# Query, key and value products of two chunks at a time, with seven block products in place of eight

## The chip, the core and the metric

The kernel runs on one core of a Trainium2 chip. The metric is the device time of one execution in microseconds (us), from the first to the last instruction on the core. TensorE is called PE here, VectorE DVE, ScalarE ACT, GpSimd POOL; SP is the engine whose queue issues nearly all transfers.

## What is computed

A two-layer encoder over 2048 frames of 1024 features, in float32. Cut to what matters:

```python
# layer A: pooling mixer, output projection, gated embedding
x = x + pool_mixer(rms_norm(x, a_norm), a_w_in, a_w_group, a_scale, a_w_out)
x = x + (p[0] @ ple_w[0]) * sigmoid(x @ ple_gate_w[0])
# layer B: one key/value projection, queries, stick-breaking attention
k, v = split(rms_norm(x, kv_norm) @ w_kv)          # 1024 -> 1024 each
q, z = split(rms_norm(x, b_norm) @ b_w_in)         # 1024 -> 1024 each
k, q = rms_norm(heads(k), k_norm), rms_norm(heads(q), b_q_norm)   # 16 heads of 64
beta = sigmoid(q @ k.T / 8)                        # strictly causal
A[t, s] = beta[t, s] * prod(1 - beta[t, j] for s < j < t)
x = x + ((A @ v) * silu(z)) @ b_w_out
x = x + (p[1] @ ple_w[1]) * sigmoid(x @ ple_gate_w[1])
```

## The kernel before, in words

The 2048 frames are four chunks of 512 (`NSUB`, `W5`). Every dense product is done in three matmuls: the activations and the weights are each split into a rounded high part and the rest (`split`, `put_split`: ACT casts the high part, DVE or POOL subtracts it), and high·high, low·high and high·low are summed in PSUM.

**Weights** come in units of 256 columns by two row blocks, or 512 columns by one, in a fixed order (`plan`). `pump` loads the next unit as soon as one of nine buffers (`UNITS`, line 29) is given back, so loads run up to nine units ahead of PE. A unit is 12 matmuls of work. The first time a unit is used its raw form (256 KB) is loaded and split on the chip; where it will be used again its split form (512 KB) is stored (`once`, `keep=True`) and loaded from there later.

**One chunk's front half**: `mixer` (mixer products; in chunk 0 also `fold`, which multiplies weights together), `out_steps` (output projection), `gate_steps` (gate and embedding), `gate_z` and `kvq`. `kvq` (line 690) makes q, k or v of one half of the columns: activations stand still as 128 x 128 blocks and 512 weight columns stream, 8 row blocks x 4 token blocks x 3 matmuls. Per chunk that is 3 kinds x 2 halves x 96 = 576 matmuls. `keyed` (line 757) then scales a token block of k or q by its norm, sums squares per head, takes the power -1/2 on POOL (`rsqrt_mean`, line 162; 8 heads, so 8 columns at a time) and multiplies; after the fourth token block four jobs `finish(m)` are put in `lag`, the first due 34 PE steps later, in which PE transposes the rows and the result is split and stored. `valued` and `differences` store v and make differences of neighbouring rows.

**Attention** goes by slots (chunk, head, key chunk), two half-steps each. In a half-step PE does `gather` (matmuls of weights `at` with `vv` into `pso`), `turn` (8 transposes of an older half-step's `pp` into `psa`), `front` (4 matmuls into `psl`); ACT makes the sigmoid `pp` and the high part of `at`; DVE subtracts for the low part of `at` (line 984) and runs the product scan over `pp` (line 964), two of each per half-step. `turn` lags `front` by three half-steps and `gather` lags by four, so what `turn` of one half-step starts is used by `gather` in the next. A slot on the diagonal has scans of 128, 256, 384 and 512 columns; any other has four of 512.

**Order.** `stream()` is one generator of dense matmuls: the front half of chunk 0, then per chunk the rest of q, k, v and the front half of the next chunk, and at the end `post` (output projection and gate) of chunks 0 to 2. Attention starts when the first half of chunk 0's heads are there; from then on each half-step is followed by a number of dense matmuls from that stream (`rate`, `fill`), so that attention of chunk c runs beside the dense work of the next one. The last `post` runs alone. Instructions are put on each engine in program order where it is held (`keep_in_program_order`, `state["hold"]`); elsewhere a scheduler places them. Each engine, and SP with its transfers, goes strictly through its own list.

Of the kernel before, what the change touches and what calls it, by code (L numbers as in the profile page):

```python
# [32 lines left out]
def f(ap):  # L33
    return ap.bitcast(F32)


@with_exitstack
def trunk_kernel(ctx, tc, x, p, a_norm, wu_t, wz_a, w_group, a_scale, a_w_out, kv_norm, w_kv,
# [41 lines left out]

    def timed(gen):
        for _ in gen:
            pass_time()
            yield

# [11 lines left out]
    neghalf = cp.tile([P, 8], F32, name="neghalf")  # L97
# [43 lines left out]
    row = flat("row", 6)  # L141
# [4 lines left out]
    pair = lambda nm: pool.tile([P, 2, W5], F32R, tag="act", name=nm, bufs=16)  # L146
# [25 lines left out]
    def split(pr, src, lo, n=0):  # L172
        high = lambda: A.copy(out=pr[:, 0], in_=src)
        low = lambda: lo.tensor_tensor(out=pr[:, 1], in0=src, in1=f(pr[:, 0]), op=ALU.subtract)
        if n and not state["solo"]:
            late(n, high, low)
        else:
            high()
            low()
# [71 lines left out]
    PAIRS = [(0, 1), (2, 3), (4, 5), (6, 7)]  # L251

# [4 lines left out]
    def plan_wide(nm, src, b, gain, keep):  # L257
        for kt in range(KT):
            plan.append(((nm, b, kt), src[b], (kt,), W5, gain, keep))

    def plan_kvq(s, b):
        keep = s >= b
        plan_wide("q", b_w_q, b, g_b, keep)
        plan_wide("k", w_kv, b, g_kv, keep)
        plan_wide("v", w_kv, 2 + b, g_kv, keep)
# [11 lines left out]
    for s in range(NSUB):  # L277
# [10 lines left out]
        if s:  # L288
            plan_kvq(s, 0)
        for b in range(4):  # L290
            plan_block("zb", b_w_z, b, g_b, True)
        if not s:
            plan_kvq(s, 0)
        plan_kvq(s, 1)
        if s == 0:
            first_chunk = len(plan)
# [3 lines left out]
    def product(ps, us, acts, c0, back):  # L300
        n = len(acts)
        i = 0
        for u, kts in us:
            settle(u)
            for e, kt in enumerate(kts):
                hi, lo = (u[:, l, e, c0 : c0 + P] for l in range(2))
                T.matmul(ps, hi, acts[kt][:, 0], start=(i == 0), stop=False)
                yield
                T.matmul(ps, hi, acts[kt][:, 1], start=False, stop=False)
                yield  # L310
                i += 1
                T.matmul(ps, lo, acts[kt][:, 0], start=False, stop=(i == n))
# [4 lines left out]
    def product2(pss, us, acts):  # L317
# [3 lines left out]
        for part, back in ((us[:-1], False), (us[-1:], True)):  # L321
            for k in range(2):
                for u, kts in part:
                    settle(u)
                    for e, kt in enumerate(kts):
                        hi, lo = (u[:, l, e, k * P : k * P + P] for l in range(2))
                        T.matmul(pss[k], hi, acts[kt][:, 0], start=(i[k] == 0), stop=False)
                        yield
                        T.matmul(pss[k], hi, acts[kt][:, 1], start=False, stop=False)
                        yield  # L330
                        i[k] += 1
                        T.matmul(pss[k], lo, acts[kt][:, 0], start=False, stop=(i[k] == n))
                        yield
# [70 lines left out]
    def gather_squares(ck, nm, o, src):  # L404
        if o == 0:
            ck[nm] = pool.tile([P, W5], F32, tag="acc", name="acc", bufs=1)
# [87 lines left out]
    def prep(s):  # L494
        ck = chunk[s]
        ck["x"] = []
        for o in range(KT):
            xin = io("xin")
            nc.sync.dma_start(out=xin, in_=x[o * P : (o + 1) * P, s * W5 : (s + 1) * W5])
            pr = pair("xp")  # L500
# [152 lines left out]
    def gate_steps(x1, ple, put, ahead=lambda: None):  # L653
        for b in range(4):
# [6 lines left out]
            for k in range(2):  # L661
                o = 2 * b + k
# [17 lines left out]
    lag = []  # L680

    STEPS = []
    for j in (0, 2):
        STEPS += [(j, kt) for kt in range(4)]
        STEPS += [(j + i, kt + 4 * (1 - i)) for kt in range(4) for i in (1, 0)]
        STEPS += [(j + 1, kt) for kt in range(4, KT)]

    FIRST_STEPS = [(j, kt) for kt in range(KT) for j in range(2)] + STEPS[16:]

    def kvq(s, kind, b):  # L690
        ck = chunk[s]
        us = take(KT)
        banks, early = {}, []
        for j, kt in STEPS if "r2" in ck else FIRST_STEPS:
            tk = slice(j * P, (j + 1) * P)
            if kt == 0:
                banks[j] = dense()
            u = us[kt][0]
            settle(u)
            for xh, wh in ((0, 0), (1, 0), (0, 1)):  # L700
                T.matmul(banks[j], ck["x2"][kt][:, xh, tk], u[:, wh, 0], start=(kt == 0 and xh == wh),
                         stop=(kt == KT - 1 and wh == 1))
                if j == 3 and wh:
                    give_back()
                yield
            calm = state["solo"] or 7 <= state["since"] <= state["until"] - 3
            if lag and calm and time["now"] >= max(state["next"], lag[0][0]):
                lag.pop(0)[1]()
                state["next"] = time["now"] + 9
            if kt < KT - 1:  # L710
                continue
            done = [(j, banks.pop(j))]
            if "r2" not in ck:
                qs = row("qs")
                A.copy(out=qs, in_=done[0][1])
                early.append((j, qs))
                if j == 0:
                    continue
                ck["r2"] = token_norm(ck["acc2"], "y")
                if s:  # L720
                    lag.append((time["now"] + 20, lambda: ck.update(rb2=bcast(ck["r2"], "y"))))
                done = early
            if kind == "v" and j == 3:
                while lag:
                    lag.pop(0)[1]()
            for i, ps in done:
                rj = ck["r2"][:, i : i + 1]
                (valued if kind == "v" else keyed)(s, kind, b, i, ps, rj)

    def valued(s, kind, b, j, ps, rj):  # L730
        vr = row("vr")
# [436 lines left out]
```

## Time and profile before

| | |
|---|---|
| median of 3 runs | 2715.3 us (2714.67 to 2720.52) |
| span of the profiled execution | 2715.1 us |
| PE busy | 2681.0 us (99%), 13406 matmuls |
| DVE, ACT, POOL busy | 1770.8, 1324.4, 915.0 us |
| moved by transfers | 675.81 MB, mean 249 GB/s |
| last `fold` ends, first attention matmul, last attention front | 106.7, 372.8, 2606.8 us |
| attention stretches of chunks 0, 1, 2, 3 | 373 to 827, 846 to 1374, 1380 to 1947, 1952 to 2607 us |

The profiled execution's own time is its span. A row of the groups of instructions gives line, engine, operation, output<-input, shape and count, then the time in which any of them ran, the mean ns of one, and the engine's idle time just before them with what ended it. A row of the table by stretches gives the stretch, its length, and each engine's busy us with its number of instructions; behind them stand PE's granted clock (1.00 is full), the busy share of the 16 transfer engines and GB/s. Matmuls overlap: one takes some 390 ns from start to end, but starts follow each other faster.

### The profile page before, as it was taken

The page shows a single profiled execution, that of the slowest core. Times are in us where ns is not written, and L with a number is a line of the kernel's source. Part 1 is how long each engine was busy: PE and PEld are TensorE (multiplying, and loading weights), DVE is VectorE, ACT ScalarE, POOL GpSimd, SP SyncE. Part 2 cuts the span into 40 slices and gives each one's busy share as a digit, 9 for nine tenths or more (in the row PEclk, how much of TensorE's full clock was granted, in tenths as well). Part 3 has the DMA queues.
Part 4 walks back from the last instruction along what each step waited for, and adds up shares of the span by engine and source line. Part 5 has one row for each costly group of instructions (what it writes and reads, how often), then busy time and mean ns, then how long its engine had stood idle before and what let it go on. Part 6 is the DMA issues. An engine that isn't in the chain of part 4 may idle for free.

```text
span 2715.1 us, 38035 instructions
## 1 busy us (share of the span) xinstructions
PE 2681.0 (99%) x13406; PEld 2246.7 (83%) x13406; DVE 1770.8 (65%) x2271; ACT 1324.4 (49%) x2638; POOL 915.0 (34%) x745
## 2 busy tenths in 40 slices
PE   9999999999999999999999999999999999999999
PEld 7888778888887888888878888888888888888887
DVE  6736454544355866655568878766678788788742
ACT  5435563335555344564545455554655555454531
POOL 1345564324645423464453222242242101001102
PEclk9999999999999999999999999999999999999999
DMA  7789788676899878789796665687586666667555
GB/s 249 268 314 361 286 257 284 228 248 221 290 334 318 269 256 272 244 276 374 245 308 199 219 218 181 222 283 232 176 268 220 225 212 196 221 198 252 190 165 176
DMA packets 304411, 675.81 MB, mean 249 GB/s; under 512 B 46431, under 2 KB 79199, under 8 KB 304221
## 3 DMA queue, kind: packets, MB, share of 16 engines
q1 hardware_dynamic: 303644, 672.59, 72.9%
q8 instruction: 106, 1.74, 0.3%
q10 hardware_dynamic: 576, 0.79, 0.1%
q14 instruction: 85, 0.69, 0.1%
HBM read 485.05 MB, written 188.22 MB: 248 GB/s over the span
## 4 chain that ended last, share of the span: by engine, by line
PE 85%; DMA 5%; DVE 3%; POOL 2%; ACT 2%; issue 2%; SPq 1%; ACTq 0%; DVEq 0%; POOLq 0%
PE psd L47 57%; PE pso L47 9%; PE psl L47 9%; PE psa L51 8%; DMA xin<-in_x_dram 1%; DMA wpair<-once 1%; PE pst L51 1%; POOL rq L166 1%; DMA wraw<-in_gate_a_dram 1%; DMA wraw<-in_b_w_q_dram 1%; DVE us L536 1%; DVE pp L964 1%; SPq L66 0%; DVE at L984 0%; DMA wraw<-in_a_w_out_dram 0%
## 5 line engine op out<-in xcount | busy, mean ns | idle before, releaser
L964 DVE TENSOR_TENSOR_SCAN pp<-pp,floor 128x512 f32<-128x512 f32 (+3 forms) x640 | 754.7, 1216 | 5.7 <-ACT pp L960 4.7
L984 DVE TENSOR_TENSOR at<-psa,at 128x512 fp32r<-128x512 f32 (+3 forms) x640 | 361.5, 604 | 363.1 <-ACT at L982 361.7
L47 PE MATMUL psd<-wpair,x 128*128 128x512 f32 x2304 | 563.8, 395 | 5.9 <-ACT wpair L199 2.8
L47 PE MATMUL psd<-x,wpair 128*128 128x512 f32 x2304 | 550.9, 390 | 1.2 <-DVE sg L674 1.1
L982 ACT CAST at<-psa 128x512 fp32r<-128x512 f32 (+3 forms) x640 | 303.2, 524 | 503.5 <-PE psa L51 500.7
L47 PEld LDWEIGHTS psd<-x,wpair 128*128 128x128 f32 x2304 | 430.9, 188 | 92.6 <-DVE sg L674 1.5
L47 PEld LDWEIGHTS psd<-wpair,x 128*128 128x128 f32 x2304 | 427.3, 189 | 96.2 <-ACT wpair L199 4.0
L47 PE MATMUL psd<-xp,wpair 128*128 128x512 f32 x1536 | 362.5, 391 | 1.3 <-DMA wpair<-once 1.1
L47 PEld LDWEIGHTS psd<-xp,wpair 128*128 128x128 f32 x1536 | 286.5, 188 | 62.3 <-DMA wpair<-once 1.5
L47 PE MATMUL pso<-at,vv 128*128 128x512 f32 (+3 forms) x1280 | 313.9, 364 | 5.9 <-DVE at L984 5.9
L960 ACT ACTIVATE pp<-psl 128x512 f32<-128x512 f32 (+3 forms) x640 | 312.9, 548 | 1.6 <-PE psl L47 1.2
L51 PE MATMUL psa<-ident,pp 128*128 128x128 f32 x2176 | 291.9, 274 | 0.8 <-ACT rby L388 0.8
L47 PEld LDWEIGHTS pso<-at,vv 128*128 128x128 f32 x1280 | 230.7, 188 | 58.0 <-DVE at L984 10.2
L51 PEld LDWEIGHTS psa<-ident,pp 128*128 128x128 f32 x2176 | 252.9, 141 | 29.3 <-ACT rby L388 1.0
L47 PE MATMUL psl<-kk,qa 128*128 128x512 f32 (+3 forms) x640 | 257.4, 407 | 0.0
L47 PE MATMUL psl<-kk,qb 128*128 128x512 f32 (+3 forms) x640 | 233.4, 365 | 0.6 <-ACT qb L927 0.6
L47 PE MATMUL psd<-og,wpair 128*128 128x512 f32 x744 | 181.6, 391 | 1.3 <-ACT own L998 1.3
L47 PE MATMUL psd<-mp,wpair 128*128 128x512 f32 x768 | 179.3, 390 | 0.0
L1007 POOL TENSOR_TENSOR os<-os,zt 128x512 f32<-128x512 f32 x32 | 52.7, 1648 | 356.9 <-ACT os L1006 321.3
L47 PEld LDWEIGHTS psd<-mp,wpair 128*128 128x128 f32 x768 | 143.7, 188 | 30.2
L47 PEld LDWEIGHTS psd<-og,wpair 128*128 128x128 f32 x744 | 138.9, 188 | 31.3 <-ACT own L998 1.7
L664 POOL TENSOR_TENSOR xj<-x 128x512 f32<-128x512 f32 x64 | 103.3, 1618 | 146.6 <-DVE sg L675 86.8
(120 smaller groups left out, 2894.9 us busy)
## 6 DMA issues: line engine op xcount, KB each, us to landing
wpair<-once SPq DMA_DIRECT2D x468, 512.0 KB, 5.2
once<-wpair SPq DMA_DIRECT2D x116, 512.0 KB, 5.8
kk<-kd SPq DMA_DIRECT2D x160, 256.0 KB, 3.7
vv<-vd SPq DMA_DIRECT2D x160, 256.0 KB, 3.9
wpair<-wf SPq DMA_DIRECT2D x48, 512.0 KB, 6.5
once<-kp SPq DMA_DIRECT2D x36, 512.0 KB, 4.2
qd<-hl SPq DMA_DIRECT2D x64, 256.0 KB, 4.1
qa<-qd SPq DMA_DIRECT2D x64, 256.0 KB, 4.5
```

The source lines that it names most:

```text
L47: return held_in_order(nc.tensor.matmul(*a, **k))
L51: return held_in_order(nc.tensor.transpose(*a, **k))
L166: G.tensor_tensor(out=out_ap, in0=ms, in1=neghalf[:, 0:w], op=ALU.pow)
L536: V.tensor_tensor(out=us[:, lo:][:, ::-1], in0=cur[:, lo:][:, ::-1], in1=cur[:, lo - sh : n][:, ::-1], op=ALU.add)
L664: G.tensor_tensor(out=xj, in0=f(x1[o][:, 0]), in1=f(x1[o][:, 1]), op=ALU.add)
L960: A.activation(out=pp[:, r0:], in_=ps[:, :w], func=AF.Sigmoid, scale=-1.0)
L964: V.tensor_tensor_scan(out=pp[:, r0:][:, ::-1], data0=pp[:, r0:][:, ::-1], data1=least, initial=1.0 if st["diag"] else st["carry"][j], op0 ...
L982: A.copy(out=at[:, 0, cs], in_=pt[:, cs])
L984: return lambda: V.tensor_tensor(out=at[:, 1, cs], in0=pt[:, cs], in1=f(at[:, 0, cs]), op=ALU.subtract)
L1007: G.tensor_tensor(out=os, in0=os, in1=zt, op=ALU.mult)
```

## The change

**The products.** q, k and v of two chunks are made together. The two chunks are the two rows of a 2 x 2 block matrix A (1024 frames x 1024 features), the weights a 2 x 2 block matrix B, and the four result blocks come from seven block products in place of eight (the variant of Strassen's scheme with shared sums). For each kind the sums of weight blocks (four of the seven) are made once, in `mixtures`, and stored in device memory as raw float32 (`mixed`); the sums of activation blocks are made in `build` before each pair's products. `job` runs the products in the order p1, p2, p6, p3, p5, p7, p4 of 48 matmuls each, for v, then k, then q: three kinds x 336 = 1008 matmuls per pair of chunks, 2016 in all for 2304. Four PSUM banks (`total`) sum up over p1, p6, p7 and p4; p2, p3 and p5 have two banks of their own (`own`), and `evacuate` adds the parts. Weights of the products are no longer stored split.

**The norm.** q, k, v and z are made of already scaled activations (`scaled`). In `keyed` the power is taken once for four token blocks, 32 columns at a time, and `finish` is due 44 steps later.

**The order.** `opening` runs the front halves of chunks 0 and 1 and the pair's products with nothing beside them; `attend` runs the 48 attention slots of chunks 0 and 1 beside chunk 2's front half and chunk 3's mixer and output projection (1584 dense matmuls); `middle` runs chunk 3's gate and the second pair's products alone; a second `attend` runs the 112 slots of chunks 2 and 3 beside `gate_z(3)` and three `post` (1488 dense matmuls).

```diff
-    row = flat("row", 6)
+    row = flat("row", 11)
...
+    KINDS = "vkq"
+    PRODUCTS = ("p1", "p2", "p6", "p3", "p5", "p7", "p4")
+    WHOLE = {"p1": (0, 0), "p2": (0, 4), "p3": (1, 4)}
...
+    def mixtures():
+        turn = 0
+        for kind in KINDS:
...
+            for i in range(4):
+                w = [ppt("mx") for _ in range(4)]
+                for n, t in enumerate(w):
+                    nc.sync.dma_start(out=t, in_=src[b0 + n % 2][:, i + n // 2 * 4])
+                yield
+                for n, t in enumerate(w):
+                    kt = i + n // 2 * 4
+                    A.activation(out=t, in_=t, func=AF.Identity, scale=gain[:, kt : kt + 1])
+                b11, b12, b21, b22 = w
+                eng = (V, G)
+                eng[turn % 2].tensor_tensor(out=b11, in0=b12, in1=b11, op=ALU.subtract)
...
+                for name, t in (("p5", b11), ("p6", b22), ("p7", b12), ("p4", b21)):
+                    store(16, out=mixed[kind, name][:, i], in_=t)
...
+    def job(c0, c1):
+        for kind in KINDS:
+            totals, parts = [], {}
+            for name in PRODUCTS:
+                us = take(4)
+                for j in range(4):
...
+                    apart = name in ("p2", "p3", "p5")
+                    ps = bank("psl", "own") if apart else totals[j]
+                    for i, (u, _) in enumerate(us):
+                        settle(u)
+                        for xh, wh in ((0, 0), (1, 0), (0, 1)):
+                            T.matmul(ps, half_of(sets[name][i], xh)[:, tk], u[:, wh, 0],
...
+                    evacuate(c0, c1, kind, name, j, totals[j], ps, parts)
...
+        if name == "p2":
+            copy("c11", own)
+            add("c11", total)
+            done(c0, 0, parts.pop(("c11", j)))
...
-    def keyed(s, kind, b, j, ps, rj):
+    def keyed(s, kind, b, j, qs):
...
+        V.tensor_reduce(out=ss[:, 8 * j : 8 * j + 8], in_=sq.rearrange("q (h d) -> q h d", d=HD), op=ALU.add, axis=AX.X)
         rows.append(qs)
         if j < 3:
             return
+        rq = pool.tile([P, 32], F32, tag="rq", name="rq")
+        rsqrt_mean(rq, ss, HD, "q")
+        for i, qs in enumerate(rows):
+            q8 = qs.rearrange("q (h d) -> q h d", d=HD)
+            V.tensor_tensor(out=q8, in0=q8, in1=rq[:, 8 * i : 8 * i + 8].unsqueeze(2).to_broadcast([P, 8, HD]),
+                            op=ALU.mult)
...
         for m in range(4):
-            lag.append((time["now"] + 34, lambda m=m: finish(m)))
+            lag.append((time["now"] + 44, lambda m=m: finish(m)))
...
+    def opening():
+        yield from mixed_part(0)
+        yield from gated_part(0, prep(1), 22)
+        yield from mixed_part(1, mixtures(), 42)
+        yield from gated_part(1, prefill(0), 26)
+        settled_lag()
+        yield from pair_part(0, 1)
...
+    attend(0, FIRST, beside_first(), lambda n: (1584.0 - 44) / (2 * FIRST + LAG_G + 1))
...
+    alone(middle())
+    attend(FIRST, len(slots), beside_second(),
+           lambda n: (1488.0 - 44) / (2 * (len(slots) - FIRST) + LAG_G + 1))
```

The instructions stand in three places as follows. **First, SP's transfers** during chunk 0's output projection. Before: `wraw` are raw weights loaded for PE, `once` split weights stored, `xr` the residual.

```order
L210 DMA wraw<-in_a_w_out_dram 128x512
L66 DMA once_1744<-wpair 128x1024
L210 DMA wraw<-in_a_w_out_dram 128x512
L610 DMA xr<-in_x_dram 128x512 x2
L66 DMA once_1748<-wpair 128x1024
L610 DMA xr<-in_x_dram 128x512
L66 DMA once_1752<-wpair 128x1024
L210 DMA wraw<-in_a_w_out_dram 128x512
L66 DMA once_1756<-wpair 128x1024
```

In the changed kernel, at the same place; `mx` are the weight blocks of `mixtures`, `mixedv`, `mixedk` and `mixedq` their stored sums.

```order
L225 DMA wraw<-in_a_w_out_dram 128x512
L70 DMA once_1666<-wpair 128x1024
L225 DMA wraw<-in_a_w_out_dram 128x512
L70 DMA once_1678<-wpair 128x1024
L880 DMA mx<-in_w_kv_dram 128x512
L70 DMA mixedvp_375<-mx 128x512
L70 DMA mixedvp_373<-mx 128x512
L70 DMA mixedvp_376<-mx 128x512
L70 DMA mixedvp_374<-mx 128x512
L225 DMA wraw<-in_a_w_out_dram 128x512 x2
L880 DMA mx<-in_w_kv_dram 128x512
L639 DMA xr<-in_x_dram 128x512
```

The code puts `mixtures` beside chunk 1's mixer; the scheduler has moved it forward. All 48 loads `mx` and 46 of the 48 stores `mixed` stand between the last `fold` of chunk 0 and the load of the first weights of chunk 1's mixer, among chunk 0's own weights.

**Second, PE** where k or q is transposed (`pst<-ident,qs`). Before, in chunk 0's `kvq`:

```order
L47 MATMUL psd<-wpair,x_2291 128x512 x3
L51 MATMUL pst<-ident,qs 128x128 x2
L47 MATMUL psd<-wpair,x_2343 128x512 x2
L47 MATMUL psd<-wpair,x_2564 128x512 x2
L47 MATMUL psd<-wpair,x_2343 128x512
L47 MATMUL psd<-wpair,x_2564 128x512
```

In the changed kernel, in the first pair's k; the 48 `own` are product p2, whose rows are the first to be transposed, the `total` behind them p6.

```order
L51 MATMUL own<-wpair,xs 128x512 x48
L51 MATMUL total<-wpair,xs 128x512 x44
L55 MATMUL pst<-ident,qs 128x128 x4
L51 MATMUL total<-wpair,xs 128x512 x4
L51 MATMUL own<-wpair,xs 128x512 x5
L55 MATMUL pst<-ident,qs 128x128 x4
```

There the scheduler had freedom and put transposes singly where their rows were due; now the place is held in program order: exactly 44 matmuls after the product's last one. This comes seven times for a pair of chunks before its attention begins (p2, p5, p7 and p4 of k; p2, p5 and p7 of q), 14 times in all; the four transposed rows of p4 of q fall into the attention stretch.

**Third, PE** in the last attention stretch, in a half-step with full slots beside the same output projection (`psd<-og,wpair`). Before:

```order
L47 MATMUL pso<-at,vv 128x512 x4
L51 MATMUL psa<-ident,pp 128x128 x8
L47 MATMUL psl<-kk,qa 128x512
L47 MATMUL psl<-kk,qb 128x512
L47 MATMUL psl<-kk,qa 128x512
L47 MATMUL psl<-kk,qb 128x512
L47 MATMUL psd<-og,wpair 128x512 x12
```

In the changed kernel:

```order
L51 MATMUL pso<-at,vv 128x512 x4
L55 MATMUL psa<-ident,pp 128x128 x8
L51 MATMUL psl<-kk,qa 128x512
L51 MATMUL psl<-kk,qb 128x512
L51 MATMUL psl<-kk,qa 128x512
L51 MATMUL psl<-kk,qb 128x512
L51 MATMUL psd<-og,wpair 128x512 x6
```

Each half-step of attention has 6 or 7 dense matmuls beside it where it had 11 or 12.

More of the change, by code (lines that the diff above doesn't have):

```diff
@@ L96, in trunk_kernel @@
                     fill=1.0, base=0, channel_multiplier=1)
-    neghalf = cp.tile([P, 8], F32, name="neghalf")
+    neghalf = cp.tile([P, 32], F32, name="neghalf")
     V.memset(neghalf, -0.5)
@@ L676, in gate_steps, with valued @@
                 put(o, sg)
[L680 to L731, printed above, removed]
-        A.activation(out=vr, in_=ps, func=AF.Identity, scale=rj)
+    def valued(s, b, j, vr):
         vs = tmp("vs")
@@ L816, in put, with gate_z @@
+    def gate_z(s, acts):
+        def put(o, ps):
+            sg, zr = tmp("sg"), tmp("zr")
+            high = lambda: A.activation(out=sg, in_=ps, func=AF.Sigmoid)
+            mult = lambda: V.tensor_tensor(out=zr, in0=ps, in1=sg, op=ALU.mult)
+            if state["solo"]:
+                high()
+                mult()
+            else:
+                late(4, high, mult)
             store(24, out=zd[s][o], in_=zr)
-        first = []
-        if "r2" not in ck:
+        for b in range(4):
```

422 lines of the change are left out of this document (262 added, 160 removed).

## Prediction

> **What bounds the kernel now.** I read the page's busy shares and chain first.
>
> ```profile
> span 2715.1 us, 38035 instructions
> PE 2681.0 (99%) x13406; PEld 2246.7 (83%) x13406; DVE 1770.8 (65%) x2271; ACT 1324.4 (49%) x2638; POOL 915.0 (34%) x745
> PE 85%; DMA 5%; DVE 3%; POOL 2%; ACT 2%; issue 2%; SPq 1%; ACTq 0%; DVEq 0%; POOLq 0%
> ```
>
> PE is busy all but 34 us and carries 85% of the chain, so fewer matmuls shorten the span one for one, unless something else becomes the later one in the stage concerned. DVE's 65% and the transfers' 249 GB/s are means, and the change alters how work is spread over the stages; so I next read stretches (length, then busy us with instructions of PE, PEld, DVE, ACT, POOL, then clock, transfer share, GB/s).
>
> ```profile
> 107.00:227.00 120.00, 119.89 (x530) 98.92 (x529) 61.85 (x84) 49.42 (x91) 63.50 (x50) 1.00 0.86 310
> 200.00:300.00 100.00, 99.98 (x448) 82.69 (x447) 57.63 (x81) 54.86 (x101) 53.05 (x40) 1.00 0.94 343
> 300.00:400.00 100.00, 93.23 (x436) 75.37 (x435) 50.77 (x59) 58.13 (x98) 63.77 (x55) 1.00 0.83 267
> 800.00:900.00 100.00, 96.92 (x476) 80.72 (x475) 60.28 (x75) 54.23 (x105) 51.24 (x44) 0.98 0.94 331
> 1225.00:1275.00 50.00, 50.00 (x251) 42.10 (x250) 31.80 (x37) 24.04 (x51) 25.62 (x20) 1.00 1.04 388
> 1400.00:1500.00 100.00, 95.79 (x480) 79.66 (x479) 91.04 (x109) 47.75 (x101) 37.59 (x34) 0.98 0.68 226
> 1952.00:2607.00 655.00, 653.29 (x3420) 551.22 (x3419) 523.17 (x621) 336.99 (x689) 114.85 (x77) 1.00 0.66 218
> ```
>
> Two resources are nearly used up somewhere. In 107 to 227 us (chunk 0's output projection and gate) the transfer engines are 86% busy while PE has no gap. In 1400 to 1500 us, where attention stands thickest, DVE is 91% busy, and there PE falls to 96%: DVE's bursts reach it. The change adds transfers to the first and thins the dense work beside attention in the last.
>
> **Part by part.** The profiled execution's span is 2715.1 us, 0.2 from the median of 2715.3; I sum against 2715.1.
>
> *Fewer matmuls.* A matmul's mean of 395 ns overlaps the next one's; the pace is in the chain (start, length, what).
>
> ```profile
> 739.91 12.27 PE psd L47 x54
> ```
>
> 12.27 / 54 = 0.227 us. 2304 - 2016 = 288 matmuls fewer: 288 x 0.227 = 65.4 us, all on PE's path.
>
> *Waits inside the old products.* The stretch 300:400 holds the first k and q and leaves PE idle 6.8 us; 800:900 leaves 3.1, 1400:1500 leaves 4.2. The waits by name (total us, count, longest):
>
> ```profile
> PE pso L47 <- DVE at L984: 5.9, 6, 2.6
> PE pst L51 <- DVE qs L767: 5.4, 3, 2.8
> ```
>
> Transposes waiting for normed rows (`pst`) are about half of it. These places no longer exist; I take 6.8 + 3.1 + half of 4.2 = -12. What comes in their place is priced next but one.
>
> *The mixtures' transfers.* All loads and 46 of 48 stores of `mixtures` land in the stage that now takes 107 to 227 us. Its transfers by 40 slices of 3 us, and one of its groups (count, KB each, us to landing):
>
> ```profile
> DMA packets 14182, 37.23 MB, mean 310 GB/s; under 512 B 1569, under 2 KB 1569, under 8 KB 14174
> GB/s 26 355 354 312 352 411 267 69 210 388 361 369 191 305 399 193 317 317 298 280 20 277 353 298 293 296 333 415 410 371 412 358 266 324 368 410 302 335 390 404
> wraw<-in_b_w_z_dram SPq DMA_DIRECT2D x8, 256.0 KB, 6.0
> ```
>
> The stage moves 37.2 MB. The eight loads for z (2.1 MB) leave it, and 96 transfers of 256 KB (25.2 MB) come: 60.3 MB. What do full engines move? 310 / 0.86 = 360 GB/s here, 343 / 0.94 = 365 in 200:300, 388 / 1.04 = 373 in 1225:1275. At 360 the stage lasts 60.3 / 0.360 = 167 us where PE needs 120: 47 us. SP issues all of it in one list, so PE's next weight loads queue behind stores whose sums POOL or DVE have not made yet; buffered weights (eight units of 256 KB, 2.1 MB, or 6 us of transfers) can be ahead. +41. Ends: 60.3 / 0.412 - 120 - 6 = +20 if the best single slices are held, and 60.3 / 0.343 - 120 - 6 = +50 at the rate of 200:300. POOL's part does not decide: 24 of the 48 subtractions at
>
> ```profile
> L174 POOL TENSOR_TENSOR xp<-xin,xp 128x512 fp32r<-128x512 f32 x24 | 31.4, 1310 | 48.0 <-ACT xp L173 47.7
> ```
>
> 1.3 us are 31 beside its 63.5 of 120.
>
> The Trainium skill ("Perfetto Trace Analysis", Roofline) says that a core active alone is bounded by its 16 transfer engines at about 435 GB/s; by that the term would be 60.3 / 0.435 - 126 = 13 us, an estimate. The trace stays under it, 415 GB/s in its best 3 us here, and 388 over 50 us.
>
> *The norm's chain.* Transposes come exactly 44 matmuls behind the product: 44 x 0.227 = 10.0 us, held in PE's order, so everything behind waits if the rows are late. The chain, by its nearest rows:
>
> ```profile
> L715 ACT COPY qs<-psd 128x512 f32<-128x512 f32 x6 | 3.3, 582 | 2.2 <-PE psd L47 2.2
> L630 DVE TENSOR_TENSOR xr<-psd,xr 128x512 f32<-128x512 f32 x64 | 43.1, 679 | 42.2 <-PE psd L47 26.8 <-issue 4.7 <-DMA wraw<-in_a_w_out_dram 4.4
> L762 ACT ACTIVATE sqq<-qs 128x512 f32<-128x512 f32 x64 | 40.1, 631 | 1.4
> L765 DVE TENSOR_REDUCE ssq<-sqq 128x8 f32<-128x512 f32 x64 | 43.3, 681 | 80.6 <-ACT sqq L762 80.6
> L165 POOL TENSOR_SCALAR ms<-ss 128x4 f32<-128x4 f32 x8 | 1.8, 222 | 68.8 <-ACT ss L399 68.6
> L165 POOL TENSOR_SCALAR ms<-ssq 128x8 f32<-128x8 f32 x64 | 21.2, 331 | 116.4 <-DVE ssq L765 113.5
> L166 POOL TENSOR_TENSOR r<-ms,neghalf 128x4 f32<-128x4 f32 x8 | 9.1, 1133 | 0.7
> L166 POOL TENSOR_TENSOR rq<-ms,neghalf 128x8 f32<-128x8 f32 x64 | 110.8, 1731 | 4.4
> L767 DVE TENSOR_TENSOR qs<-qs,rq 128x512 f32<-128x512 f32 x64 | 60.3, 942 | 48.2 <-POOL rq L166 47.9
> ```
>
> No row has 32 columns. From 4 to 8 columns the power grows from 1.13 to 1.73, 0.15 a column: 1.73 + 24 x 0.15 = 5.3 at 32 (ends 1.7, if flat, and 6.9, if proportional); the mean before it 0.33 + 24 x 0.027 = 1.0. The four multiplications cost 0.94 each, or 0.68 like a plain DVE operation in this list; I take 0.81, 3.2 together. For p2: 0.58 + 0.68 + 0.63 + 0.68 + 1.0 + 5.3 + 3.2 = 12.1, late by 2.1; p5, p7 and p4 have no copy ahead of an addition, 11.5, late by 1.5. Four groups are of p2, ten of the others: 4 x 2.1 + 10 x 1.5 = +23. Ends: 0 if the power is flat (chain 8.5 at most); with 6.9 and 0.94, late by 4.2 and 3.6: +53. Queued behind the waiting transposes is all of the running product; waiting for them, the stores of k and q.
>
> *The second attention stretch.* DVE and PE by tile in 1952:2607 (scans and their `pp`; the products `at`; dense `psd`; columns as above, where an engine without instructions is left out):
>
> ```profile
> 1952.00:2607.00 655.00, 121.52 (x922) 107.03 (x920) 308.04 (x254) 130.09 (x255) 1.00 0.66 218
> 1952.00:2607.00 655.00, 130.42 (x508) 92.80 (x508) 150.88 (x255) 127.19 (x256) 1.00 0.66 218
> 1952.00:2607.00 655.00, 353.29 (x1450) 270.73 (x1451) 32.14 (x48) 18.57 (x30) 1.00 0.66 218
> ```
>
> Before, this stretch has 64 slots (48 full with four scans of 512, 16 diagonal with 1280 columns in all): 118784 columns. Now it has chunk 2's 48 too: 204800, x 1.724. DVE: (308.04 + 150.88) x 1.724 = 791, the rest 523.17 - 458.92 = 64 about as it is plus 17 for another chunk's head rows and z: 872 us. PE: attention is 655 - 1450 x 0.227 = 326, x 1.724 = 562, and 1488 - 44 = 1444 dense x 0.227 = 328: 890 us. DVE would be 98% busy where it was 80%. One half-step with its engines' times in order (start, length, count):
>
> ```profile
> 2440.20 1.29 DVE L984 TENSOR_TENSOR at<-psa,at 128x512 fp32r<-128x512 f32 x2 [0.94 <-ACT at L982]
> 2441.41 2.45 DVE L964 TENSOR_TENSOR_SCAN pp<-pp,floor 128x512 f32<-128x512 f32 x2
> 2445.48 1.29 DVE L984 TENSOR_TENSOR at<-psa,at 128x512 fp32r<-128x512 f32 x2 [1.62 <-ACT at L982]
> ```
>
> 5.28 us a half-step with about 11 dense matmuls; with 6 of them 5.28 - 5 x 0.227 = 4.14. DVE needs 1.29 + 2.45 = 3.74 and its other work (81 us over 224 half-steps, 0.36): 4.10. So nothing is left, and each delay of DVE's reaches PE's `gather`. At 91% busy the row 1400:1500 lost 4%; part of that is the products' own. I take 3% of the 80 full slots' time (160 half-steps x 4.14 = 662): +20. Ends: 0 (PE three to four half-steps behind its DVE work absorbs all), +70 (third rival). The first stretch has 1584 dense matmuls beside 48 thinner slots, and DVE stays near its 80%.
>
> *At nothing.* The 20 splits of `build` go to POOL:
>
> ```profile
> L174 POOL TENSOR_TENSOR x<-xr,x 128x512 fp32r<-128x512 f32 x32 | 45.6, 1426 | 261.3 <-ACT x L173 261.3
> ```
>
> 20 x 1.43 = 29 us, behind the 192 matmuls of `gate_z` (43.6 us) and 96 of p1 and p2 (21.8); uncovered it would cost 7 us a pair. The evacuations have PSUM banks of their own.
>
> **Sum:** 2715.1 - 65.4 - 12 + 41 + 23 + 20 = 2721.7, or 2722.
>
> **The rivals.** *Transfers keep up (faster).* If the engines hold the 412 GB/s that single slices show, the first term is 20: 2701. For it: 411, 415, 412 and 410 in the slices. Against: 50 us at 388 is the best long row. It decides from 60.3 / (120 + 6 + 27) = 394 GB/s, where the sum passes 2709. By the Trainium skill's bound named above (Roofline) the time would be 2694; the rows have not reached that rate.
>
> *The power costs by instruction (faster).* If 32 columns take 1.7 us like 8, all 14 groups are in time: 2722 - 23 = 2699. The rows of 4 and 8 columns speak against a flat price, but give only two points.
>
> *DVE sets the second stretch's pace (slower).* If PE's order and DVE's, locked half-step to half-step, let DVE be busy 91% at most, as 1400:1500 shows where attention stood thickest, the stretch lasts 872 / 0.91 = 958 instead of 890: +68 instead of 20, 2770. For it: the half-step above, 4.10 against 4.14. Against: PE's 99.7% in 1952:2607 at 80% of DVE. It decides once DVE's share cannot pass 95% (872 / 0.95 = 918, 28 us).
>
> That the change doesn't do what it says is out: the order of the changed kernel has 2016 products.
>
> **How the numbers follow.** Forecast 0.45, own range 2700 to 2745 (mixtures 35 to 50, the other terms off by ten or so each way); transfers keep up 0.22; flat power 0.13; DVE's pace 0.20. Both faster rivals together give 2678, all low ends together 2658; the range begins halfway, 2668. Its top lies halfway between DVE's pace, 2770, and that with the transposes at their upper end, 2800: 2785. A measurement of this kernel tells 0.2% from no change: below 2709.9 is faster, above 2720.7 slower. Faster: 0.45 x 0.25 + 0.22 x 0.8 + 0.13 x 0.85 = 0.40. The same: 0.45 x 0.22 + 0.22 x 0.12 + 0.13 x 0.1 = 0.14. Slower: the rest, 0.46.
>
> **What would show it.** In the changed profile: 2016 products of q, k and v; in chunk 0's output and gate stage a transfer share near 1, PE idle by 35 to 50 us with weights as its releaser, SP's list behind `mixed`; `rq` of 32 columns at 5.3 us and `pst` waiting for `qs` 14 times by 1.5 to 2; the second stretch near 910 us with DVE at 95 to 98% and `pso` waiting for `at` some 20 us. A stage without PE gaps while `mixed` is stored, a power of under 3 us, or a second stretch above 950 us makes the step concerned wrong.

## The result and the profile after

The changed kernel takes 2846.9 us (median of 4 runs, 2840.6 to 2849.9); the kernel before takes 2715.1 (4 runs). The ratio is 1.0477, interval 1.0460 to 1.0493: slower by 132 us, where I had forecast slower by 7, outside my range of 2668 to 2785. The profiled execution of the changed kernel, the fastest of its four, has a span of 2838.6 us, 123.5 more than the one before. Its page, with busy time by engine and the chain:

```profile
span 2838.6 us, 38319 instructions
PE 2696.2 (95%) x13118; PEld 2215.0 (78%) x13118; DVE 1946.6 (69%) x2479; ACT 1431.3 (50%) x2838; POOL 1038.0 (37%) x737
PE 37%; DVE 8%; POOL 3%; issue 3%; DMA 3%; ACT 2%; SPq 0%; POOLq 0%; DVEq 0%; ACTq 0%
```

PE has 288 matmuls fewer and yet is busy 15 us longer; 142 us of the span it is not busy at all, against 34 before. PE's part of the chain fell from 85% to 37%. Where, the stretches tell (columns as in the prediction): chunk 0's output and gate, the first pair's products, the first attention stretch, the second pair's products, the second attention stretch.

```profile
107.20:264.50 157.30, 134.24 (x523) 103.66 (x521) 77.92 (x91) 80.20 (x132) 104.80 (x80) 0.92 1.01 382
502.00:806.70 304.70, 270.74 (x1154) 214.86 (x1153) 141.72 (x172) 144.79 (x251) 194.83 (x125) 0.95 0.64 198
806.70:1376.40 569.70, 550.78 (x2822) 458.97 (x2821) 456.90 (x580) 333.28 (x723) 225.89 (x174) 0.99 0.78 266
1504.10:1809.20 305.10, 270.95 (x1154) 215.56 (x1153) 139.24 (x171) 140.36 (x242) 185.89 (x118) 0.94 0.66 208
1809.20:2720.50 911.30, 889.13 (x4787) 743.08 (x4786) 836.40 (x1014) 558.97 (x1162) 127.80 (x73) 0.99 0.57 189
```

The two rows of products are the surprise: 305 us each, with no engine but PE above 64% and the transfers at two thirds. To compare stages I worked out a loss for each: the spacing of PE's instructions, start to start, is summed over the stage, and from it is taken what the same instructions take at the median spacing of their kind in the kernel before (0.227 us for a dense matmul). By this the kernel before loses 36 us in all and the changed kernel 225; the work itself shrinks from 2672 to 2607.

| us | forecast | measured |
|---|---|---|
| 288 matmuls fewer | -65 | -65 |
| chunk 0's output and gate | +41 | +39 |
| the pairs' products (two) | +23 | +110 (55 + 55) |
| attention, less the old products' waits | +20 - 12 = +8 | +38 (68 now, 30 before) |
| sum | +7 | +122, and 2 in small parts |

### The profile page after: what moved, and what is told of

Same layout as the page of the kernel before. It is cut to its first block, busy times and chain, and to the rows that moved or that the text cites. A ratio compares the mean times of both kernels' runs of the same rounds, so it can differ in the third digit from the quotient of the medians.

```text
span 2838.6 us, 38319 instructions
## 1 busy us (share of the span) xinstructions
PE 2696.2 (95%) x13118; PEld 2215.0 (78%) x13118; DVE 1946.6 (69%) x2479; ACT 1431.3 (50%) x2838; POOL 1038.0 (37%) x737
## 4 chain that ended last, share of the span: by engine, by line
PE 37%; DVE 8%; POOL 3%; issue 3%; DMA 3%; ACT 2%; SPq 0%; POOLq 0%; DVEq 0%; ACTq 0%
PE psd L51 18%; PE pso L51 6%; PE psa L55 6%; PE psl L51 6%; DVE pp L1102 4%; DVE at L1122 2%; POOL rq L181 1%; DMA vraw<-qs 1%; POOL xs L189 1%; PE own L51 1%; POOL wpair L210 1%; DVE qs L748 1%; DMA vs<-vraw 0%; ACT at L1120 0%; DVE sg L704 0%
## 5 line engine op out<-in xcount | busy, mean ns | idle before, releaser
L51 PE MATMUL psd<-x,wpair 128*128 128x512 f32 x1728 | 441.5, 399 | 18.7 <-ACT sg L700 7.7
L51 PEld LDWEIGHTS psd<-x,wpair 128*128 128x128 f32 x1728 | 328.5, 192 | 96.4 <-ACT sg L700 9.2
L51 PE MATMUL pso<-at,vv 128*128 128x512 f32 (+3 forms) x1280 | 329.2, 371 | 36.6 <-DVE at L1122 32.5
L51 PE MATMUL psd<-xp,wpair 128*128 128x512 f32 x1248 | 304.3, 392 | 0.4 <-DVE wpair L215 0.2
L51 PE MATMUL total<-wpair,xs 128*128 128x512 f32 x1152 | 286.5, 405 | 5.5 <-DVE zr L804 4.2
L51 PEld LDWEIGHTS psd<-xp,wpair 128*128 128x128 f32 x1248 | 231.8, 188 | 51.0 <-DVE wpair L215 1.4
L51 PEld LDWEIGHTS total<-wpair,xs 128*128 128x128 f32 x1152 | 222.1, 196 | 53.5 <-DVE zr L804 5.0
L51 PE MATMUL own<-wpair,xs 128*128 128x512 f32 x864 | 215.1, 405 | 17.6 <-ACT qs L901 11.2
L51 PEld LDWEIGHTS own<-wpair,xs 128*128 128x128 f32 x864 | 166.7, 196 | 57.4 <-ACT qs L901 15.0
L51 PE MATMUL psd<-og,wpair 128*128 128x512 f32 x744 | 187.7, 392 | 0.0
```

The source lines that it names most:

```text
L51: return held_in_order(nc.tensor.matmul(*a, **k))
```

## Experiments

Each run was timed beside the kernel before on the same chip (2716.8 to 2719.1 us there); the table gives its median and the interval of the ratio of the two. All changes are to the changed kernel. Behind them stands the loss by stage in us, worked out as above: gate of chunk 0; chunk 1's front half with `gate_z`; first pair's products; first attention; second pair's products; second attention. e7 and e9 have none, since they add matmuls of no use.

| kernel | median us | ratio's interval | gate 0 | chunk 1 | pair 1 | att. 1 | pair 2 | att. 2 |
|---|---|---|---|---|---|---|---|---|
| changed | 2846.9 | 1.046-1.049 | 39 | 3 | 55 | 32 | 55 | 36 |
| e1 later transposes | 2820.4 | 1.034-1.040 | 38 | 3 | 45 | 34 | 44 | 37 |
| e2 power by 8 | 2807.3 | 1.030-1.036 | 41 | 3 | 39 | 34 | 32 | 38 |
| e3 later casts | 2847.2 | 1.044-1.050 | 40 | 2 | 62 | 36 | 48 | 39 |
| e4 mixtures pinned | 2828.1 | 1.037-1.043 | 9 | 19 | 56 | 35 | 52 | 37 |
| e5 = e1, e2, e4 | 2773.3 | 1.017-1.024 | 8 | 19 | 23 | 42 | 29 | 35 |
| e6 = e5, split weights kept | 2786.4 | 1.022-1.029 | 9 | 19 | 59 | 34 | 7 | 41 |
| e7 useless products, 20 | 2847.8 | 1.043-1.053 | - | - | - | - | - | - |
| e8 subtractions on POOL | 2831.7 | 1.039-1.045 | 39 | 2 | 59 | 30 | 53 | 28 |
| e9 useless products, 36 | 2845.8 | 1.045-1.051 | - | - | - | - | - | - |
| e10 = e5, e8, part kept | 2751.3 | 1.009-1.017 | 8 | 15 | 33 | 35 | 13 | 30 |
| e11 = e10, more on POOL | 2747.5 | 1.008-1.015 | 8 | 20 | 32 | 34 | 13 | 22 |

### The norm's chain: e1, e2

What to explain is PE's waiting inside the products. PE's groups in the first pair's stretch of the changed kernel (busy, mean ns, idle just before and what ended it), and the new power:

```profile
L51 PE MATMUL total<-wpair,xs 128*128 128x512 f32 x576 | 144.4, 408 | 3.3 <-DVE zr L804 2.7 <-POOL wpair L210 0.7
L51 PE MATMUL own<-wpair,xs 128*128 128x512 f32 x432 | 106.2, 401 | 6.6 <-DVE qs L897 3.4 <-ACT qs L901 3.2
L55 PE MATMUL pst<-ident,qs 128*128 128x128 f32 x100 | 21.6, 305 | 24.0 <-DVE qs L748 23.5
```

```profile
L181 POOL TENSOR_TENSOR rq<-ms,neghalf 128x32 f32<-128x32 f32 x16 | 87.2, 5451 | 1.1
```

The power costs 5.45 us, close to my 5.3; yet the transposes wait 24 us in this pair and 21 in the second, twice my 23 for both. Theory A: the rows' own chain is too long for its 10 us. Theory B: it stands still in queues that hold casts of weights not yet landed. The timeline of the first group (start, length, what, wait) speaks for both:

```profile
611.62 3.01 PE L51 MATMUL own<-wpair,xs 128*128 128x512 f32 x12 [0.75 <-ACT qs L901]
...
617.34 0.72 ACT L214 ACTIVATE wpair<-wraw,gains 128x512 fp32r<-128x512 f32 x1 [2.60 <-DMA wraw<-in_w_kv_dram]
617.97 0.57 ACT L901 COPY qs<-own 128x512 f32<-128x512 f32 x1
...
621.28 0.68 DVE L740 TENSOR_REDUCE ssq<-sqq 128x8 f32<-128x512 f32 x1
...
622.37 1.29 POOL L210 TENSOR_TENSOR wpair<-wraw,wpair 128x512 fp32r<-128x512 f32 x1 [5.33 <-ACT wpair L208]
623.75 0.22 POOL L180 TENSOR_SCALAR ms<-ssq 128x32 f32<-128x32 f32 x1
624.05 5.43 POOL L181 TENSOR_TENSOR rq<-ms,neghalf 128x32 f32<-128x32 f32 x1
629.51 3.55 DVE L748 TENSOR_TENSOR qs<-qs,rq 128x512 f32<-128x512 f32 x4 [7.55 <-POOL rq L181]
631.40 2.19 PE L55 MATMUL pst<-ident,qs 128*128 128x128 f32 x4 [5.85 <-DVE qs L748]
```

Product p2 ends at 614.6. Its last block is copied only at 617.97, since ACT, which takes its list in order, had first to wait 2.60 us for a weight's transfer; then the mean waits for POOL, which was subtracting a weight, from 621.96 to 623.75. These 5 us stand in no step of my chain: the last row is ready at 633.06, 18.4 us behind the product, where I had 12.1. The seven groups of a pair are not alike. Those behind p2 of k and p5 of q wait 6.2 and 7.2 us in this pair (6.4 and 4.7 in the second); the other five wait 0.7 to 2.9 (0.5 to 3.9), near the 1.5 to 2.1 of my forecast. e1:

```diff
-            lag.append((time["now"] + 44, lambda m=m: finish(m)))
+            lag.append((time["now"] + 60, lambda m=m: finish(m)))
```

> Transposes of k and q stand 60 matmuls behind their product instead of 44, 3.6 us more room. Theory A (the rows' own chain, with one power of 32 columns, 5.45 us, is longer than the 10.0 us it was given): PE's 45 us of waiting at the transposes fall to about 8, its slower pace after waits to a half, some 50 us less, about 2795. Theory B (the chain stands still in ACT's and POOL's queues behind casts of weights whose transfers have not landed, so that it is late by 5 us or more wherever it matters): only the small waits go, some 15 us less, about 2830.

e2:

```diff
-        if j < 3:
-            return
-        rq = pool.tile([P, 32], F32, tag="rq", name="rq")
-        rsqrt_mean(rq, ss, HD, "q")
...
+        rq = pool.tile([P, 8], F32, tag="rq", name="rq")
+        rsqrt_mean(rq, ss[:, 8 * j : 8 * j + 8], HD, "q")
+        q8 = qs.rearrange("q (h d) -> q h d", d=HD)
+        V.tensor_tensor(out=q8, in0=q8, in1=rq.unsqueeze(2).to_broadcast([P, 8, HD]), op=ALU.mult)
+        if j < 3:
+            return
```

> The power is taken after each token block, 8 columns at a time, as in the kernel before; transposes stay at 44. The last block's power ends 3.7 us earlier. Theory A: the waits at the transposes fall from 45 us to about 8, some 50 us less, about 2795. Theory B: 10 to 20 us less, 2830; the transposes behind p2 of k and of q still wait 3 us or more.

Measured: 2820.4 and 2807.3. Both edits give the rows about 3.7 us more, e1 by waiting longer, e2 by an earlier end. The transposes' waits in the first pair, e1 then e2:

```profile
L55 PE MATMUL pst<-ident,qs 128*128 128x128 f32 x96 | 19.4, 306 | 15.7 <-DVE qs L748 15.4
```

```profile
L55 PE MATMUL pst<-ident,qs 128*128 128x128 f32 x100 | 16.0, 276 | 11.5 <-DVE qs L745 11.5
```

Both lie between the theories. The shorter power took 40 us off the two pairs, so the batched power is a large part; but neither edit took the waits to 8 us for both pairs, as theory A alone wanted (e2 leaves 11.5 and 6.2), and in e2 waits of 2.7, 3.4 and 5.4 us stay at three groups of the first pair. The waits for evacuations (`own`, `total`) did not shrink.

### The weights' casts: e3, e6

e3 casts weights later, when they should have landed:

```diff
-            after(5, lambda: settle(pr))
+            after(24 if state["hold"] and state["solo"] else 5, lambda: settle(pr))
```

with the same delay for the units that `gain` scales, which were cast at once.

> In the products of a pair, a weight unit is cast and subtracted 24 matmuls (5.4 us) behind the issue of its load instead of 5 or none, so that ACT, DVE and POOL reach it once it has landed. Theory B: the 23 us in which own and total products wait for evacuations go, and the transposes behind p2 come 3 us earlier: 40 us less, about 2805. Theory A: up to 10 us less, about 2837.

Measured 2847.2, no change: 7 us lost in the first pair, 8 won in the second. Theory B in this form fell. A later cast still stands in the same list, nearer to the products that need it; that this is why nothing was gained is not shown. e6 takes the casts away instead, for the second pair alone, on top of e5 (below):

```diff
-                        plan.append(((kind, name, i), src[b0 + b], (k0 + i,), W5, gain, False))
+                        plan.append(((kind, name, i), src[b0 + b], (k0 + i,), W5, gain, True))
...
-                        plan.append(((kind, name, i), mixed[kind, name], (i,), W5, None, False))
+                        plan.append(((kind, name, i), mixed[kind, name], (i,), W5, None, True))
```

> As the combination, and the split form of the pair's weights is stored in the first pair and loaded in the second, so that the second pair's products have no casts and subtractions of weights on ACT, DVE and POOL. If evacuations wait behind those casts, the second pair's waits of own and total fall from 16 us to 3 or less and its products from about 275 to 260 us, while the first pair's stay; if they wait for something else, both pairs stay alike. The first pair stores 44 MB more, some 370 GB/s in all over its 280 us with what it moves now: it may lose up to 20 us.

Second pair, PE's groups in e5 and then in e6:

```profile
L51 PE MATMUL total<-wpair,xs 128*128 128x512 f32 x576 | 140.4, 401 | 4.7 <-POOL wpair L210 2.6 <-DVE zr L802 1.5 <-DVE qs L895 0.6
L51 PE MATMUL own<-wpair,xs 128*128 128x512 f32 x432 | 106.5, 401 | 8.8 <-ACT qs L899 7.8 <-DVE qs L895 0.9
L55 PE MATMUL pst<-ident,qs 128*128 128x128 f32 x96 | 15.6, 281 | 4.6 <-DVE qs L745 4.6
```

```profile
L51 PE MATMUL total<-wpair,xs 128*128 128x512 f32 x576 | 136.8, 394 | 2.1 <-DMA wpair<-once 2.1
L51 PE MATMUL own<-wpair,xs 128*128 128x512 f32 x432 | 103.3, 394 | 1.4 <-DMA wpair<-once 1.3
L55 PE MATMUL pst<-ident,qs 128*128 128x128 f32 x96 | 14.4, 272 | 0.0
```

Without casts every wait for an evacuation or for a normed row is gone, 18.1 us to 3.5, and the stage's loss falls from 29 to 7 us. So the splitting of raw weights, in the same in-order lists as the evacuations and the norms, holds those up: shown for the second pair. The edit takes away the casts, the subtractions and their waits for raw weights together; which of the three counts most it does not tell. The price stands in the first pair, which stores the split form (first and second pair of e6):

```profile
488.10:796.60 308.50, 271.34 (x1150) 216.43 (x1149) 143.49 (x176) 140.60 (x242) 206.45 (x165) 0.92 0.97 339
1496.80:1752.80 256.00, 252.56 (x1150) 206.57 (x1149) 93.56 (x121) 92.84 (x159) 158.27 (x133) 1.00 0.93 320
```

Its transfers reach a share of 0.97 and its loss grows from 23 to 59: more than is won.

### What a wait costs beyond itself: e7, e9

The page of the changed kernel has a granted clock of 0.95 and 0.94 in the products. Around the wait of the first group, in the changed kernel:

```profile
622.00:625.00 3.00, 3.00 (x15) 1.00 0.56 183
625.00:628.00 3.00, 0.55 (x3) 1.00 0.18 65
628.00:631.00 3.00, 0.00 (x0) 0.82 0.00 0
631.00:634.00 3.00, 2.28 (x6) 0.50 0.26 87
634.00:637.00 3.00, 3.00 (x9) 0.55 0.00 0
637.00:640.00 3.00, 3.00 (x19) 1.00 0.69 186
```

(PE's busy time and count, then clock, share, GB/s.) When PE goes on, its clock is 0.50, and matmuls follow each other at 0.427 us instead of 0.227 until about 637. To see whether standing still does this, both runs put products of no use into the wait:

```diff
+            if m == 0 and s % 2 == 0 and (kind, b) in (("k", 0), ("q", 1)):
+                fill = half_of(sets["p2"][0], 0)
+                for _ in range(36):
+                    T.matmul(pt.rearrange("q j t -> q (j t)"), fill[:, 0:P], fill, start=True, stop=True)
```

This is e9; e7 had 20 of them, behind p2 of k and of q.

> The changed kernel with 20 products of no use put ahead of the transposes behind p2 of k and of q, in the place of four waits of 4.4 to 6.1 us. They delay nothing that is not waiting (4.5 us). If PE's slower pace behind these waits (0.427 us a matmul, clock 0.50) comes from PE's having stood still, it goes: 3 us at each, 12 us less, about 2827, with more work. If it has another cause, the time stays at 2839 or grows.

e7 gave 2847.8 and decides nothing: I had put one of the two fills at the wrong group (the second long wait is behind p5 of q), and behind p2 of k 20 products left 1.2 us of waiting and two short waits of 0.27 between the transposes, after which the clock was 0.58 all the same.

> The changed kernel with 36 products of no use (8.2 us) ahead of the transposes behind p2 of k and behind p5 of q, the two places in each pair where PE in the changed kernel stands 5.9 to 8.6 us in all, the gaps between the four transposes counted. If standing still is what halves PE's clock, the products behind them follow each other at 0.227 us and not 0.427, the granted clock there is 1.00, and the time is up to 6 us less, about 2835. If not, 0.427 and 0.50 stay.

e9, the same place, which it reaches some 2.7 us later:

```profile
628.00:631.00 3.00, 3.00 (x14) 1.00 0.10 38
631.00:634.00 3.00, 3.00 (x15) 1.00 0.02 5
634.00:637.00 3.00, 3.00 (x17) 1.00 0.25 87
637.00:640.00 3.00, 3.00 (x17) 1.00 0.00 0
```

The four transposes and what follows, in e9's timeline:

```profile
636.23 0.60 PE L55 MATMUL pst<-ident,qs 128*128 128x128 f32 x4
```

They take 0.60 us in place of 2.19, the clock stays at 1.00 and the products behind run at 0.227 us: the halved clock comes from PE's standing still. The Trainium skill ("TensorE: Matmul & The Clock Gate", Part 1) tells of such a gate, closed by idleness and opened by about 3.4 us of work; the 0.50 and the time until 637 agree. The total, 2845.8, did not fall as I expected: the first pair is 304.5 us long against 304.7, with 72 x 0.227 = 16.3 us of useless products in it. Those took the place of 12 us of waiting (the transposes of the pair wait 12.4 us in place of 24.0), and about what they took beyond it the full clock gave back.

### The mixtures' transfers: e4

```diff
-                    nc.sync.dma_start(out=t, in_=src[b0 + n % 2][:, i + n // 2 * 4])
+                    tc.keep_in_program_order(nc.sync.dma_start(out=t, in_=src[b0 + n % 2][:, i + n // 2 * 4]))
```

> The loads of the mixtures are pinned to their place in SP's program order, which spreads them and their stores over chunk 1's mixer, output projection and gate. Same bytes. If the transfer engines set the end of chunk 0's output and gate stage, that stage falls from 162 to about 122 us, and at most 10 us come back later: about 2815. If ACT's and POOL's splits of weights set it, it falls by 10 us at most: about 2837.

Measured 2828.1. The stage, then chunk 1's mixer, output and gate, then `gate_z`:

```profile
107.20:236.40 129.20, 122.40 (x531) 100.04 (x530) 53.37 (x69) 48.42 (x86) 79.20 (x63) 0.99 0.84 297
236.40:425.10 188.70, 188.70 (x842) 155.74 (x842) 110.67 (x128) 61.95 (x105) 94.32 (x79) 1.00 1.00 370
425.10:488.30 63.20, 52.23 (x206) 39.76 (x205) 52.62 (x59) 29.87 (x59) 38.37 (x28) 0.89 0.69 244
```

With the bytes spread, the stage's loss falls from 39 to 9 us. The edit takes the mixtures' work on the engines along (ACT has 86 instructions there where it had 132), so by itself it does not part the two; but the transfers' share was 1.01 through the whole stage, and with that it is they that set its end. Chunk 1's stage takes them at a share of 1.00 without a gap of PE, but 16 us come back in `gate_z`, more than I expected.

### Together, and attention: e5, e8, e10, e11

e5 joins e1, e2 and e4.

> Three edits together: the power 8 columns at a time, transposes 60 matmuls behind, the mixtures' loads pinned. Theory A: with 3.6 us more room on top of the shorter chain the 17.7 us left at the transposes fall to about 3 and the slower pace after them goes too, 25 us less than with the shorter power alone, and the pinned loads give 13: about 2767. Theory B: the transposes left waiting are held up by ACT and POOL and gain little, about 2785; in both the 32 us of waits for evacuations stay.

2773.3, between the theories and nearer A: with both edits the pairs lose 23 and 29 us instead of 55 each, the transposes wait 4.0 and 4.6.

e8 moves 28 subtractions off DVE while attention runs:

```diff
-                split(pr, xr, V if k else G, 7)
+                split(pr, xr, V if k and state["solo"] else G, 7)
...
-            split(pr, pin, V)
+            split(pr, pin, V if state["solo"] else G)
```

> The changed kernel with 28 subtractions of about 1.0 us, of the output projection's and the embedding's splits beside attention, moved from DVE to POOL (10 in the first stretch, 18 in the second). If DVE's work sets the second stretch's pace, its 928 us fall by 10 to 18 us; if PE's own order does, or POOL's operations lengthen DVE's scans by as much, nothing.

2831.7; the second stretch's loss falls from 36 to 28 us, a little less than the 10 us that I expected at the least. e10 adds this to e5, keeps the split form of p3, p5 and p6 only, and takes a mixture every 32 matmuls.

> The combination of e5, with the subtractions of e8 on POOL, the split form of p3, p5 and p6's weights kept for the second pair (18.9 MB stored in the first, 70 GB/s on top of its 211), and the mixtures taken every 32 matmuls in place of 42. From 2774: 9 less in attention, 10 less in the second pair, the first pair as it was if its transfers keep up, up to 5 less at gate_z: about 2750, still behind the kernel before.

2751.3. The first pair loses 10 us more than in e5, the second 16 less; the earlier mixtures move their cost from `gate_z` (15 us in e5, 1 now) into chunk 1's output projection (0 in e5, 14 now). e11 moves two more kinds of addition:

```diff
-                V.tensor_tensor(out=sg, in0=sg, in1=xj, op=ALU.add)
+                (V if state["solo"] else G).tensor_tensor(out=sg, in0=sg, in1=xj, op=ALU.add)
...
-            V.tensor_tensor(out=os[mine], in0=own[mine], in1=os[mine], op=ALU.add)
+            G.tensor_tensor(out=os[mine], in0=own[mine], in1=os[mine], op=ALU.add)
```

> As e10, and POOL also takes the additions of the heads' halves (32 beside the second stretch, 0.7 us each on DVE) and the last addition of the gate beside attention (about 1.07 us each, 24 in the second stretch). If DVE sets attention's pace, 15 us less than e10; if POOL's operations lengthen the scans by as much as they take off, the same time or more.

2747.5; against e10 the difference of the medians is inside their scatter, but the second stretch's loss falls from 30 to 22 us. From the first to the last attention front of the second stretch, e8 and then e11:

```profile
1807.30:2710.80 903.50, 885.52 (x4787) 740.19 (x4786) 833.04 (x996) 558.37 (x1162) 160.63 (x91) 1.00 0.59 190
```

```profile
1734.20:2631.10 896.90, 884.00 (x4790) 738.72 (x4789) 813.56 (x943) 559.25 (x1163) 236.32 (x147) 1.00 0.60 194
```

911.3, 903.5, 896.9 us with DVE at 836, 833, 814: DVE's work does delay PE there, and some of what is taken off it comes back, for the same 446 scans (`pp`) take 524, 534 and 554 us. The best of these kernels is still 1.1% (0.8 to 1.5) behind the kernel before; no version in this study beat it.

## Why the prediction was wrong

**Right: the matmuls.** The work on PE shrank by 65 us, as counted.

**Right: the mixtures.** The stage moved 60.1 MB (I had 60.3) and lost 39 us (I had 41). The engines held 382 GB/s over 157 us, more than my 360 and less than the 394 from which the faster rival would have decided (there my sum gives 2708, not the 2709 that I wrote). At 382 and with my 6 us of look-ahead the term would be 31; the look-ahead did not show, and the two errors cancel, which is luck. Of the 39 us PE stood idle 23; some 10 more are matmuls at half pace behind the waits (below).

**Right in its wait, and in its time by luck: the second stretch.** From its first to its last front it takes 911.3 us where I had 890 + 20. But by the table 36 of these are lost, so the work is 875: PE's work was 15 us less than I had, its loss 16 more, and the two cancel. What PE waited there for `at`, 21.6 us, is what I had priced:

```profile
L51 PE MATMUL pso<-at,vv 128*128 128x512 f32 (+3 forms) x880 | 232.0, 379 | 21.9 <-DVE at L1122 21.6
```

DVE is busy 836 / 911 = 92% instead of the 95 to 98 that I had named as a sign: my 872 us of DVE work was 36 too much. 92% is where the rival on DVE's pace put the limit (91%), and e8 and e11 stay at 92 and 91. So that rival's mechanism is not refuted; its 958 us came from the 872. The waits for `at` in the whole kernel:

```profile
PE pso L51 <- DVE at L1122: 32.5, 37, 2.7
```

These waits were 5.9 us in all before. Part of them lies in the first stretch, where I had said that nothing changes because DVE stays near 80%. Its 368 products with `at`, now and then the same 368 before (chunks 0 and 1):

```profile
L51 PE MATMUL pso<-at,vv 128*128 128x512 f32 (+3 forms) x368 | 88.5, 354 | 14.7 <-DVE at L1122 10.9 <-ACT at L1120 3.6
```

```profile
L47 PE MATMUL pso<-at,vv 128*128 128x512 f32 (+3 forms) x368 | 80.9, 341 | 0.0
```

DVE did stay at 80% (457 of 570 us), and PE waited all the same. Of the 30 us by which the table's row on attention is off, 16 are the second stretch's (36 for 20), so about 14 stand here: that step, "stays near its 80%" as a reason for no loss, failed too. What delays DVE there no run tells apart; I did not try it.

**Wrong: the norm's chain, +23 where the pairs' products lose 110.** The power's price was right. Two steps failed: I added the chain's durations as if each engine were free when its turn came, and I put the evacuations under "at nothing" because they have banks of their own. Of the first pair's 55 us 34 are PE's waits (24 at transposes, 10 for evacuations and weights), some 10 are 50 matmuls at about half pace with no wait of their own, and the other 11 I did not take apart. Three things were left out:

- The same in-order lists of ACT, POOL and DVE now hold the splitting of 84 raw weight units per pair, some of them waiting for their transfers. Evacuations and norms stand behind them. Taking the splitting away (e6) took every such wait away in the second pair and 22 us of its loss; casting later (e3) did not. I had read "no longer stored split" as less to transfer only. Before, all 96 units of chunks 2 and 3 came split from memory, but of the 96 of chunks 0 and 1 only 24: 72 were split on the chip there too. So for the first pair the number of splittings alone explains little, and no run took them away there; that they hold it up as they do the second pair is argued from the same waits in its timeline.
- Of the 45 us that the transposes wait in both pairs, over half stand at four of the 14 groups, those behind p2 of k and p5 of q; the other ten wait 2.1 on average, near my 1.5 to 2.1. At p5 of q it is not weights alone that stand in the lists: the changed kernel also reloads and splits activations of the second chunk there (`reload`, tiles `xw` and `x`), and in the first pair the four multiplications take 5.7 us from 771.1 on, where I had 3.2. Shortening the chain by 3.7 us (e2) took 40 us off both pairs, more than my whole term, and 27 of them are waits at the transposes. They also wait one by one for their four rows: in the changed kernel's timeline above four transposes take 2.19 us, in e9's 0.60.
- After a long wait PE often runs at half speed for some 4 us. The wait of 5.9 us cost about 2 us more, and e9 shows that standing still is the cause. The trace of before has few such waits, and I gave a wait only its own length.

## What to carry to other kernels

A chain's length is not the sum of its operations but of the places they get in each engine's list: before moving a step, look at what else the change puts into those lists, above all instructions that wait for transfers. Work saved on the busiest engine counts only as long as the others keep it supplied; here 65 us saved met 189 us of new loss. And engine shares say little about a stage in which every other engine's share is moderate and PE waits for each in turn.

## What the hardware showed

Waits as short as 2.7 us were followed by half speed, though not always. Here is one in the first pair of the changed kernel, and below it the same place in e2 (start, length, what, wait):

```profile
513.22 4.60 PE L51 MATMUL total<-wpair,xs 128*128 128x512 f32 x12 [2.69 <-DVE zr L804]
```

```profile
514.78 3.07 PE L51 MATMUL total<-wpair,xs 128*128 128x512 f32 x12 [2.67 <-DVE zr L802]
```

The Trainium skill ("TensorE: Matmul & The Clock Gate", HAM oscillation) gives the rule that idle gaps be no longer than some 3.4 us; here a shorter one was enough in one run, and the measurement decides. In the changed kernel twelve matmuls take 4.60 us where 11 spacings of 0.227 and one length of 0.39 make 2.89, and the granted clock from 514 to 524 us is 0.84; in e2 a wait as long left them at 3.07. So these runs give no length of wait that decides it. The power on POOL grows by the column: 1.13, 1.73 and 5.45 us at 4, 8 and 32. And the transfer engines held 382 GB/s, loads and stores mixed, for 157 us.
